# Where the top-k searches of a sparse-attention layer run, and which engine splits the weights beside them

## The chip, the cores and the metric

The kernel runs as one program on one core of a Trainium2 chip. The core has a matrix engine (TensorE, PE in the profile; its weight loads are PEld), a vector engine (VectorE, DVE), an activation engine (ScalarE, ACT), a general engine (GpSimd, POOL) and an engine that issues most transfers (SyncE, SP). Each engine works off its own queue in order, and semaphores hold an instruction back until its inputs and its output's place are free. The metric is the device time of one execution in microseconds (us). Products collect in PSUM, in 128-partition banks; all else lies in SBUF.

## The reference

One step of a two-layer decoder for a prompt of 1024 tokens and eight samples of one token with 1024 past positions each; both share the weights. Layer 0 (state-space and convolution branches) is not touched. Layer 1 is attention over keys that an indexer picks:

```python
def index_scores(qi, wi, ki):
    s = jnp.einsum('bthd,bsd->bths', qi, ki, preferred_element_type=jnp.float32) * IDX_DIM ** -0.5
    return jnp.einsum('bths,bth->bts', jax.nn.relu(s), wi.astype(jnp.float32) * IDX_HEADS ** -0.5)

def dsa_attend(q, qi, wi, q_pos, ki_all, gather_kv, topk):
    scores = index_scores(qi, wi, ki_all)
    ...
    _, idx = lax.top_k(scores, topk)
    ...
    p = jax.nn.softmax(logits, axis=-1)

def odd_out(x, o, z, w_out, ln_g, ln_b):
    out = (o.reshape(b, l, ATTN_WIDTH) * jax.nn.silu(z)) @ w_out
    return layer_norm(ALPHA * x + out, ln_g, ln_b)
```

For each of 1024 prompt queries and 8 sample queries, eight indexer heads score every admissible position, the 256 best are kept, and 16 heads attend to these alone. Queries, keys, values, indexer inputs and a gate z come from one projection of x.

## The kernel before

Nothing is gathered for the prompt. The kernel computes each query's 256th largest score, turns scores into a mask of 0 or a large negative number, and adds it to the logits. So layer 1 has the following stages.

- **Projections.** `mm3` multiplies 128 output columns by a chunk of 344 tokens (there are three, `CH`), in 24 matmuls: for each of eight blocks of the contraction high by high, high by low and low by high, since each fp32 operand is split into a rounded part and the rest. `load_w` fetches a projection's weights in two halves, rounds them on ScalarE (`whi`, L108) and subtracts on VectorE, or on the engine that its argument names (`wlo`, L109). Indexer keys, values and indexer queries (L996 and after, tiles `even` and `odd`) come first, then the attention's queries (`QQ`, eight), keys (`KK`, two) and gates (`ZZ`, eight; called gates below, since a Silu follows).
- **Banks.** The pools `pp`, `pt` and `pm` hold PSUM banks. `QQ` takes `pp`, `KK` and `ZZ` alternate between `pt` and `pp` through `either()`.
- **Scores.** For each block of 128 queries, in the order of `SCORE_ROWS`, and each head and 512 keys, two matmuls (L1033, L1034) fill a `pt` bank, ScalarE takes the Relu into one of two buffers, `eq` and `cum` (L1036), and VectorE multiplies by the head's weight and adds into `S` (L1040).
- **Samples' scores.** `QIP` holds the samples' indexer queries, put in place by 16 small copies (L1058, L1059). Matmuls with past keys collect in three banks `acc` (L1068, L1071), ScalarE takes the Relu (L1074, L1075), and a matmul with `W2` weighs the heads and leaves eight rows in `Ss` (L1086, L1087).
- **Searches.** A search builds the threshold from its top bit down: it counts the scores on one side of a candidate, and keeps or drops the bit. `topk_halves` ("d", query blocks 7, 6, 5) counts on VectorE (L1264) in 16 steps on the upper 16 bits and 16 on the lower. `topk_signs` counts on ScalarE by a sum of signs (L1231) and decides on GpSimd (L1236, L1250 to L1253); it runs as "a" for the blocks 4, 3 and 2, three counts in each of 32 steps, and as "s" for the samples' eight rows of 1025 scores, 32 steps more.
- **Masks.** `masks` (L1299 and after) makes masks on VectorE, for "d", "a" and "s" in this order.
- **Sample logits.** `QS` gathers sample queries by 16 copies (L1151). After each gate projection `sample_keys` fetches past keys and adds 32 matmuls (L1166) to two banks `lg`. `sample_softmax` (from L1558) later adds the mask, which two kinds of matmul (L1565, L1571) spread from 8 rows to 128.
- **Attention** over the blocks 7 down to 0 (logits L1403, maximum L1404, exponential L1408), the gate, and the output projection.

A scheduler fixes each engine's order at build time, from the order of the text and from where tiles come free in their pools. So a bank's pool or an engine's choice moves other instructions too.

Of the kernel before, what the change touches and what calls it, by code (L numbers as in the profile page):

```python
# [880 lines left out]
def layer1(k):  # L881
# [113 lines left out]
    for i in range(4):  # L995
        w = load_w(k, A["W"][QI + i])  # L996
        even, odd = (rq(F32R), rq(F32R)) if i < 3 else (qb(), qb())
        for t0, n in CH:
            p = pp(k)
            mm3(k, p, w, x1, t0, n)  # L1000
            sl = slice(t0, t0 + n)
            nc.scalar.copy(even[0:64, sl], p[0:64])
            nc.vector.tensor_tensor(even[64:128, sl], p[0:64], even[0:64, sl].bitcast(F32), op=ALU.subtract)
            nc.scalar.copy(odd[64:128, sl], p[64:128])
            nc.vector.tensor_tensor(odd[0:64, sl], p[64:128], odd[64:128, sl].bitcast(F32), op=ALU.subtract)
            if t0 + n == T:
# [48 lines left out]
    for h in range(8):  # L1055
        i, j = h // 2, h % 2
        src = qis[64 * j : 64 * j + 64, i, :]
        nc.vector.tensor_copy(QIP[0:64, h : 256 : 80], src[:, 0:8:2])  # L1058
        nc.vector.tensor_copy(QIP[64:128, 8 + h : 256 : 80], src[:, 1:8:2])  # L1059
# [22 lines left out]
    W2 = k.t(tk, [64, 8], F32, "W2")  # L1082
    nc.vector.tensor_tensor(W2, p[:64, :8], c1("bm64")[:64], op=ALU.mult)
    for hf in range(2):
        p = pt(k)
        nc.tensor.matmul(p[:8], W2, rS[:, hf * 512 : hf * 512 + 512], start=True, stop=True)  # L1086
        nc.scalar.copy(Ss[:, hf * 512 : hf * 512 + 512], p[:8])  # L1087
    p = pm(k)
    nc.tensor.matmul(p[:8, 0:8], W2, rS[:, 1024:1032], start=True, stop=True)
    sx = k.t(tk, [8, 8], F32, "sx")  # L1090
    nc.vector.tensor_tensor_reduce(out=sx, in0=p[:8, :8], in1=k.ident[:8, :8], scale=1.0, scalar=0.0,
                                   op0=ALU.mult, op1=ALU.add, accum_out=Ss[:, 1024:1025])

    lg = [pt(k) for _ in range(2)]
# [9 lines left out]
        return pt(k)[:, :344] if turn[0] % 2 else pp(k)  # L1104


    for i in range(8):
        w = load_w(k, A["W"][QQ + i])
        for t0, n in CH:
            p = pp(k)  # L1110
            mm3(k, p, w, x1, t0, n)
            hi, lo = ev(F32R), ev(F32R)
            nc.scalar.copy(hi, p)
            nc.vector.tensor_tensor(lo, p, hi.bitcast(F32), op=ALU.subtract)  # L1114
            for a, x in enumerate((hi, lo)):
                h = 4 * a + 2 * (i % 2)
                nc.sync.dma_start(dq[i // 2, h : h + 2, :, t0 : t0 + n].rearrange("h d t -> (h d) t"), x.bitcast(F32))
            if t0 + n == T:
                nc.scalar.copy(qs[:, i, :], p[:, NP - t0 : n])
    KT = [ra() for _ in range(4)]  # L1120
    for i in range(2):
        w = load_w(k, A["W"][KK + i])
        for t0, n in CH:
            p = either()
            mm3(k, p, w, x1, t0, n)
            sl = slice(t0, t0 + n)
# [21 lines left out]
    for h in range(16):  # L1148
        i, j, g = h // 2, h % 2, h // 4
        r0, o, x = 64 * (g % 2), g // 2 * 256, h % 8  # L1150
        nc.vector.tensor_copy(QS[r0 : r0 + 64, o : o + 256].rearrange("p (f x) -> p f x", f=2)[:, :, x : x + 121 : 40],  # L1151
                              qs[64 * j : 64 * j + 64, i, :].rearrange("p (f c) -> p f c", f=2))
    SL = ra(F32, "ki")[:, :NP]
    ring = [rq() for _ in range(3)]
# [11 lines left out]
                    nc.tensor.matmul(lg[i % 2][r : r + 32, j * 128 : j * 128 + 128], QS[:, o : o + 32],  # L1166
                                     kp[n][:, j, gp * 128 : gp * 128 + 128], start=False, stop=(i > 5), skip_group_check=True)
# [48 lines left out]
    def topk_signs(name, R_, bl):  # L1216
# [10 lines left out]
        for bit in range(31, -1, -1):  # L1227
            cnt = small("cnt", F32)
            for j, (s, rows, w, _) in enumerate(bl):
                jk = k.t(sc_pool, [128, 1032], BF16, "jk" + name, 1)[:rows, :w]  # L1230
                nc.scalar.activation(jk, s, AF.Sign, bias=cand.bitcast(F32)[:, j : j + 1], scale=-1.0, accum_out=cnt[:, j : j + 1])  # L1231

            def fits(out, col, m):

                for j, (_, _, w, _) in enumerate(bl):
                    eng.tensor_scalar(out[:, j : j + 1], cnt[:, j : j + 1], float(w - 2 * TOPK), m(j), op0=ALU.is_le, op1=col)  # L1236

            new = small("cand")
            low, by = small("low"), small("by")
            if bit == 31:  # L1240

                sgn = small("sgn", F32, 1)
                fits(low, ALU.add, lambda j: -1.0)
                fits(sgn, ALU.mult, lambda j: 2.0)
                eng.tensor_scalar(sgn, sgn, -1.0, None, op0=ALU.add)
                eng.tensor_tensor(fstep, fstep, sgn.unsqueeze(1).broadcast_to((R_, 31, n)), op=ALU.mult)
                eng.tensor_copy(by, fstep[:, 30, :])
                eng.tensor_tensor(new, low, by, op=ALU.add)
            else:
# [3 lines left out]
                eng.tensor_tensor(new, low, by, op=ALU.add)  # L1253
# [100 lines left out]
    s8 = [(Ss[:, :1025], 8, 1025, Ss[:, :1025])]  # L1354
# [203 lines left out]
    PT = ra(F32, "ki")[:, :NP].rearrange("p (j r) -> p j r", j=8)  # L1558

    def sample_softmax():  # L1560
        R8 = c1("r128")[:8]
        mx = k.t(right, [128, 1], F32, "mx")
        sm = k.t(right, [128, 1], F32, "sm")
        xm = pop()
        nc.tensor.matmul(xm[:, :1], R8, Ss[:, 1024:1025], start=True, stop=True)  # L1565
        nc.vector.tensor_tensor(nl, nl, xm[:, :1], op=ALU.add)
        m2 = k.t(at, [128, 2], F32, "m2", 1)
        yield
        for hf in range(2):
            lg = pop()  # L1570
            nc.tensor.matmul(lg, R8, Ss[:, hf * 512 : hf * 512 + 512], start=True, stop=True)  # L1571
# [233 lines left out]
```

## Time and profile before

| what | us |
|---|---|
| median of 3 runs | 1693.05 |
| the three runs | 1691.49 to 1696.0 |
| the profiled execution | 1691.48 |
| its span | 1689.3 |
| layer 0 | until about 900 |
| indexer keys, values and indexer queries | 900 to 1006 |
| scores, with a part of `QQ` | 1006 to 1086 |
| rest of `QQ`, `KK` | 1086 to 1190 |
| gates | 1190 to 1292 |
| attention, with output | 1292 to 1660 |
| last transfers | to 1689 |

A busy engine is one with an instruction running; its waits count as idle time and are put down to the instruction that released it. Matmuls overlap in the pipeline, so the distance between two starts is what one costs, not its duration. PEclk is the granted clock, 1.00 being full speed. A row of grouped instructions reads: line, engine, operation, output and inputs with shapes, count, then total and mean duration, then idle time in front and its releasers. A row of waits reads: who waited for whom, total us, times, the longest. A row of busy time by stage gives start and end, length, then each engine's busy time with its count.

### The profile page before, as it was taken

Reading aid. Unit: us, or ns where it says so; the run is one execution under the profiler, and the core shown is the slowest. Engines: PE = TensorE matmul, PEld = TensorE weight load, DVE = VectorE, ACT = ScalarE, POOL = GpSimd, SP = SyncE. Lnnn points to the kernel's source line nnn. Section 1 sums busy time; section 2 is a strip of 40 time slices with the busy share of each in tenths; the row PEclk is TensorE's granted clock in tenths of the full one; section 3 lists DMA queues with packets and bytes.
Section 4 is the critical chain, followed back from the end, with each engine's and each line's share of the span. In section 5 each row is a group of like instructions: output and inputs, shape, how many; then the busy total and the mean of one; then the engine's idle time right before and its main releaser. Section 6 shows DMA issues by size and latency. Waiting matters only on the chain. (4 is left out here: it accounts for less than half of the span.)

```text
span 1689.3 us, 28852 instructions
## 1 busy us (share of the span) xinstructions
PE 1592.6 (94%) x10334; PEld 1433.3 (85%) x10334; DVE 1170.9 (69%) x2484; ACT 871.2 (52%) x1960; POOL 335.7 (20%) x676
## 2 busy tenths in 40 slices
PE   8999989989999998998899999888898899999996
PEld 7999989989999997998889999878887577676674
DVE  4788987460557777766575558999966966565673
ACT  5245523552445565444534546577765755545663
POOL 4000000001222234123422200144361510112120
PEclk9999999999999998999999999999999999999998
DMA  7332243354111155433431214422345424443450
GB/s 235 110 118 62 68 113 101 129 192 140 46 34 63 65 158 184 131 113 103 151 115 53 92 46 132 126 94 95 120 147 183 129 52 117 124 110 89 99 136 37
DMA packets 167090, 186.26 MB, mean 110 GB/s; under 512 B 20484, under 2 KB 131420, under 8 KB 166692
## 3 DMA queue, kind: packets, MB, share of 16 engines
q1 hardware_dynamic: 164436, 178.68, 35.6%
q0 software_dynamic: 1216, 4.37, 0.8%
q8 instruction: 81, 1.33, 0.4%
q10 hardware_dynamic: 1296, 1.38, 0.3%
q14 instruction: 61, 0.50, 0.1%
HBM read 132.43 MB, written 54.05 MB: 110 GB/s over the span
## 5 line engine op out<-in xcount | busy, mean ns | idle before, releaser
L132 PE MATMUL pp<-act,whi 128*128 128x344 f32 x1016 | 329.8, 326 | 12.5 <-ACT act L233 8.1
L134 PE MATMUL pp<-act,wlo 128*128 128x344 f32 x1016 | 331.0, 328 | 10.9 <-DVE wlo L109 10.9
L133 PE MATMUL pp<-act,whi 128*128 128x344 f32 x1016 | 330.1, 325 | 0.9 <-POOL act L726 0.8
L132 PEld LDWEIGHTS pp<-act,whi 128*128 128x128 f32 x1016 | 193.9, 191 | 15.8 <-ACT act L233 8.1
L134 PEld LDWEIGHTS pp<-act,wlo 128*128 128x128 f32 x1016 | 194.1, 191 | 13.5 <-DVE wlo L109 11.8
L133 PEld LDWEIGHTS pp<-act,whi 128*128 128x128 f32 x1016 | 193.9, 191 | 3.2 <-POOL act L726 1.1
L108 ACT CAST whi<-wst 128x512 fp32r<-128x512 f32 x150 | 92.2, 617 | 150.5 <-PE pp L133 68.6
L334 DVE SCALAR_TENSOR_TENSOR uv<-uv,cst,uv 128x1024 f32<-128x1024 f32 x120 | 158.1, 1318 | 2.6
L109 DVE TENSOR_TENSOR wlo<-wst,whi 128x512 fp32r<-128x512 f32 x104 | 71.4, 692 | 100.9 <-ACT whi L108 100.8
L132 PE MATMUL pp<-yh,whi 128*128 128x344 f32 x412 | 135.7, 329 | 5.3 <-DVE ev L1114 3.7
L134 PE MATMUL pp<-yh,wlo 128*128 128x344 f32 x412 | 135.0, 328 | 4.1 <-DVE wlo L109 3.9
L1403 PE MATMUL lg<-w,Q 128*128 128x512 f32 (+3 forms) x384 | 104.5, 378 | 8.7 <-DVE nmx L1404 8.7
L1404 DVE CUSTOM_DVE_ANT_0 P<-lg,w 128x512 f32<-128x512 f32 (+3 forms) x144 | 82.7, 597 | 42.6 <-PE lg L1403 39.0
L109 POOL TENSOR_TENSOR wlo<-wst,whi 128x512 fp32r<-128x512 f32 x46 | 61.0, 1327 | 157.5 <-ACT whi L108 138.2
L1408 ACT ACTIVATE P<-P,mx 128x1024 f32<-128x1024 f32 (+3 forms) x64 | 63.4, 990 | 47.1 <-DVE mx L1407 43.8
L132 PEld LDWEIGHTS pp<-yh,whi 128*128 128x128 f32 x412 | 79.5, 193 | 9.2 <-DVE ev L1114 4.5
L1430 PE MATMUL tr<-cst,P 128*128 128x128 f32 x576 | 85.3, 279 | 1.8 <-DVE yo L1460 1.8
L1430 PEld LDWEIGHTS tr<-cst,P 128*128 128x128 f32 x576 | 64.9, 141 | 25.8 <-issue 18.5
L1403 PEld LDWEIGHTS lg<-w,Q 128*128 128x128 f32 x384 | 64.1, 195 | 26.6 <-DVE nmx L1404 14.5
L134 PEld LDWEIGHTS pp<-yh,wlo 128*128 128x128 f32 x412 | 79.7, 193 | 6.1 <-DVE wlo L109 5.2
L1439 PE MATMUL pv<-ph,V 128*64 128x256 f32 (+1 forms) x640 | 82.3, 372 | 2.0 <-ACT ph L1435 1.6
L1231 ACT ACTIVATE jka<-S,canda 128x640 bf16<-128x640 f32 (+2 forms) x96 | 68.7, 716 | 20.6 <-POOL canda L1253 16.0
(579 smaller groups left out, 3996.9 us busy)
## 6 DMA issues: line engine op xcount, KB each, us to landing
wst<-in_W SPq DMA_DIRECT2D x166, 256.0 KB, 3.0
Q<-dq SPq DMA_DIRECT2D x64, 256.0 KB, 4.1
dq<-ev SPq DMA_DIRECT2D x48, 172.0 KB, 1.8
q<-in_ck SPq DMA_DIRECT2D x64, 128.0 KB, 2.3
vp<-in_cv SPq DMA_DIRECT2D x64, 128.0 KB, 2.2
xst<-in_xT SPq DMA_DIRECT2D x8, 516.0 KB, 10.1
dzb<-ob SPq DMA_DIRECT2D x24, 172.0 KB, 1.8
uv<-dzb SPq DMA_DIRECT2D x8, 516.0 KB, 4.3
```

The costliest lines, as they stand in the source:

```text
L108: nc.scalar.copy(hi, st)
L109: (eng or nc.vector).tensor_tensor(lo, st, hi.bitcast(F32), op=ALU.subtract)
L132: nc.tensor.matmul(out, wh, ah, start=(start and kt == kts[0]), stop=False)
L133: nc.tensor.matmul(out, wh, al, start=False, stop=False)
L134: last = nc.tensor.matmul(out, wl, ah, start=False, stop=(stop and kt == kts[-1]))
L334: nc.vector.scalar_tensor_tensor(out, x, w[:, j : j + 1], y, op0=ALU.mult, op1=ALU.add)
L1231: nc.scalar.activation(jk, s, AF.Sign, bias=cand.bitcast(F32)[:, j : j + 1], scale=-1.0, accum_out=cnt[:, j : j + 1])
L1403: mm = nc.tensor.matmul(lg, Q[:, 4 * a + r, :], KT[g][:, s0 : s0 + m], start=(a == 0), stop=(a == 1))
L1404: nc.vector.tensor_tensor_reduce(out=P[:, s0 : s0 + m], in0=lg, in1=M[tb][:, s0 : s0 + m], scale=-0.125, scalar=BIG, op0=ALU.add, op1=ALU. ...
L1408: nc.scalar.activation(P, P, AF.Exp, bias=mx[:, r : r + 1], scale=-1.0, accum_out=rsum[:, r : r + 1])
L1430: nc.tensor.transpose(p[:, a, r * 128 : r * 128 + 128], Ps[r][:, (sb + a) * 128 : (sb + a) * 128 + 128], k.ident)
L1439: nc.tensor.matmul(pv[64 * u : 64 * u + 64, 256 * pr + c0 : 256 * pr + c1], V[:, sb + a, g * 64 : g * 64 + 64], ph[:, a, c0:c1], start=(sb ...
```

## The change

- The samples' search takes four bits at a time. The score rows are written 16 times over (128 rows: eight samples by 16 candidates, through a `W2` of 128 columns), one count tries 16 candidates, and a matmul with `same`, a 128 x 128 matrix, adds the answers of one sample. That makes 8 steps instead of 32; step n stands behind the n-th query projection. The set-up of its constants is new and stands at the start of layer 1.
- Block 4 becomes a search of its own, "a"; blocks 3 and 2 are "b". They take turns, step by step. GpSimd keeps bit values as integers (`istep`), so the copy in each step goes.
- Where both engines read a bank, ScalarE's reads come first, and VectorE's differences behind them.
- The splits of the weights (`wlo`) of `QQ` and `KK`, and the copies into `QIP` and `QS`, go to GpSimd.
- `QQ` takes its banks from `either()`.
- The mask of the samples has 128 rows, so the softmax's matmuls that spread it go. The block around `xn` moves behind the searches in the text.

The diff, cut to its core:

```diff
@@ set-up at the start of layer 1 @@
+    cix, t8, first, weight, cands = small8("cix"), small8("t8"), small8("first", I32), small8("weight"), small8("cands")
...
+    nc.gpsimd.tensor_tensor(t8, t8, c1("bm128"), op=ALU.mult)
+    nc.vector.tensor_reduce(cix, t8, axis=AX.X, op=ALU.add)
...
+    p = pm(k)[:, :128]
+    nc.tensor.matmul(p, c1("r128")[:8], c1("r128")[:8], start=True, stop=True)
+    nc.scalar.activation(same, p, AF.Copy, scale=t8[:, 3:4])
@@ samples' scores @@
-        nc.vector.tensor_copy(QIP[0:64, h : 256 : 80], src[:, 0:8:2])
+        nc.gpsimd.tensor_copy(QIP[0:64, h : 256 : 80], src[:, 0:8:2])
...
+    W2 = ev()[:64, :128]
...
-        nc.scalar.copy(Ss[:, hf * 512 : hf * 512 + 512], p[:8])
+        nc.scalar.copy(Ss[:, hf * 512 : hf * 512 + 512], p)
@@ search of the samples @@
+    def topk_samples():
...
+        for n in range(8):
+            cnt, fit, d = one("cnt"), one("fit"), one("dig")
+            nc.scalar.activation(jk[:, :1025], Ss[:, :1025], AF.Sign, bias=cand.bitcast(F32), scale=-1.0, accum_out=cnt)
+            eng.tensor_scalar(fit, cnt, float(1025 - 2 * TOPK), None, op0=ALU.is_le)
+            p = pm(k)[:, :1]
+            nc.tensor.matmul(p, same, fit, start=True, stop=True)
+            nc.scalar.copy(d, p)
...
+            yield base
@@ projections @@
     for i in range(8):
-        w = load_w(k, A["W"][QQ + i])
+        w = load_w(k, A["W"][QQ + i], eng=nc.gpsimd)
         for t0, n in CH:
-            p = pp(k)
+            p = either()
             mm3(k, p, w, x1, t0, n)
             hi, lo = ev(F32R), ev(F32R)
             nc.scalar.copy(hi, p)
+            if t0 + n == T:
+                nc.scalar.copy(qs[:, i, :], p[:, NP - t0 : n])
             nc.vector.tensor_tensor(lo, p, hi.bitcast(F32), op=ALU.subtract)
...
-            if t0 + n == T:
-                nc.scalar.copy(qs[:, i, :], p[:, NP - t0 : n])
+        ts = next(ss)
     KT = [ra() for _ in range(4)]
     for i in range(2):
-        w = load_w(k, A["W"][KK + i])
+        w = load_w(k, A["W"][KK + i], eng=nc.gpsimd)
@@ the other searches and the masks @@
-                eng.tensor_copy(low, fstep[:, max(bit - 1, 0), :])
-                eng.tensor_tensor(low, cand, low, op=ALU.subtract)
+                eng.tensor_tensor(low, cand, istep[:, max(bit - 1, 0), :], op=ALU.subtract)
...
-    a, d = blocks(ACT_ROWS), blocks(DVE_ROWS)
-    ta = topk_signs("a", 128, a)
+    a, b, d = blocks(ACT_ROWS[:1]), blocks(ACT_ROWS[1:]), blocks(DVE_ROWS)
+    sa, sb = topk_signs("a", 128, a), topk_signs("b", 128, b)
+    for n in range(32):
+        ta, tb = next(sa), next(sb)
...
-    ts = topk_signs("s", 8, s8)
     masks("d", 128, d, td)
     masks("a", 128, a, ta)
-    masks("s", 8, s8, ts)
+    masks("b", 128, b, tb)
+    masks("s", 128, [(Ss[:, :1025], 128, 1025, Ss[:, :1025])], ts)
@@ sample_softmax @@
-            nc.tensor.matmul(lg, R8, Ss[:, hf * 512 : hf * 512 + 512], start=True, stop=True)
...
-            nc.vector.tensor_tensor(x, x, lg, op=ALU.add)
+            nc.vector.tensor_tensor(x, x, Ss[:, hf * 512 : hf * 512 + 512], op=ALU.add)
```

How the scheduler puts it. On TensorE, in the last part of the scores, before (L1033 and L1034 are the scores, `pp` is a query projection):

```order
L1033 MATMUL pt_10417<-ki_9191,q_9757 128x384
L1034 MATMUL pt_10417<-ki_9192,q_9757 128x384
L132 MATMUL pp_10930<-yh_8243,whi_10858 128x344
L133 MATMUL pp_10930<-yb_8244,whi_10858 128x344
L134 MATMUL pp_10930<-yh_8243,wlo_10859 128x344
L132 MATMUL pp_10930<-yh_8221,whi_10864 128x344
L133 MATMUL pp_10930<-yl_8222,whi_10864 128x344
L134 MATMUL pp_10930<-yh_8221,wlo_10865 128x344
L1033 MATMUL pt_10423<-ki_9191,q_9758 128x384
L1034 MATMUL pt_10423<-ki_9192,q_9758 128x384
L132 MATMUL pp_10930<-yh_8225,whi_10864 128x344
```

After, from the last pair of scores on (now L1073 and L1074) through the samples' sums to the first matmul of the next projection:

```order
L1073 MATMUL pt_10478<-ki_9234,Q_9903 128x384
L1074 MATMUL pt_10478<-ki_9235,Q_9903 128x384
L1130 MATMUL pm_10571<-q_10553,ev_10563 128x8
L1108 MATMUL pt_10502<-w_10505,q_10484 64x128 x8
L1108 MATMUL pt_10502<-w_10506,q_10484 64x128 x8
L1108 MATMUL pt_10503<-w_10527,q_10484 64x128 x8
L1108 MATMUL pt_10503<-w_10528,q_10484 64x128 x8
L1127 MATMUL pt_10565<-q_10553,ev_10563 128x512
L1127 MATMUL pt_10568<-q_10553,ev_10563 128x512
L1139 MATMUL pt_10575<-ev_10577 128x512
L1139 MATMUL pt_10576<-ev_10577 128x512
L132 MATMUL pt_10593<-yh_8237,whi_10583 128x344
```

Before, the projections' matmuls stand between the score pairs to the end; now pairs follow each other, and the projections stand behind the sums.

On ScalarE at the same place, before, from one of the last Relus (L1036) to the samples' Relus (L1074) and the search "a":

```order
L1036 ACTIVATE eq_10432<-pt_10429 128x384
L1119 COPY qs_9165<-pp_10930 128x8
L1036 ACTIVATE cum_10438<-pt_10435 128x384
L1074 ACTIVATE q_10510<-pt_10459 64x512
L1231 ACTIVATE jka_12796,cnta_12791<-S_9951,canda_12789 128x384
L1231 ACTIVATE jka_12813,cnta_12812<-S_9951,canda_12798 128x640
L1074 ACTIVATE q_10510<-pt_10460 64x512
L1231 ACTIVATE jka_12815,cnta_12812<-S_9951,canda_12798 128x512
L1231 ACTIVATE jka_12817,cnta_12812<-S_9951,canda_12798 128x384
L1113 CAST ev_10999<-pp_10974 128x344
```

After, from the last Relu of the scores (now L1076) past the samples' Relus (L1114), the copies to `Ss` (L1128), and steps of both searches:

```order
L1076 ACTIVATE cum_10481<-pt_10478 128x384
L1297 ACTIVATE jka_13164,cnta_13163<-S_9994,canda_13145 128x640
L1297 ACTIVATE jkb_13001,cntb_12998<-S_9994,candb_12996 128x384
L1297 ACTIVATE jka_13185,cnta_13184<-S_9994,canda_13166 128x640
L1114 ACTIVATE q_10553<-pt_10502 64x512
L1297 ACTIVATE jka_13206,cnta_13205<-S_9994,canda_13187 128x640
L1297 ACTIVATE jkb_13026,cntb_13025<-S_9994,candb_13003 128x512
L1297 ACTIVATE jka_13227,cnta_13226<-S_9994,canda_13208 128x640
L1297 ACTIVATE jkb_13028,cntb_13025<-S_9994,candb_13003 128x384
L1114 ACTIVATE q_10553<-pt_10503 64x512
L1128 COPY Ss_9995<-pt_10565 128x512
L1297 ACTIVATE jka_13248,cnta_13247<-S_9994,canda_13229 128x640
```

Search steps have moved ahead of the samples' Relus, and there are two candidates, `canda` and `candb`, in turn.

On GpSimd during the query projections, before, only decisions of the searches "s" and "a":

```order
L1253 TENSOR_TENSOR cands_13788<-lows_13789,bys_13790 8x1
L1236 TENSOR_SCALAR bya_12869<-cnta_12860,fstepa_12757 128x1
L1251 TENSOR_TENSOR lows_13799<-cands_13788,lows_13799 8x1
L1250 CAST lows_13809<-fsteps_13738 8x1
L1253 TENSOR_TENSOR canda_12867<-lowa_12868,bya_12869 128x3
L1251 TENSOR_TENSOR lowa_12884<-canda_12867,lowa_12884 128x3
L1250 CAST lowa_12900<-fstepa_12757 128x3
L1236 TENSOR_SCALAR bys_13800<-cnts_13795,fsteps_13738 8x1
```

After, at a like place:

```order
L1317 TENSOR_TENSOR lowa_13335<-canda_13313,istepa_12915 128x1
L1319 TENSOR_TENSOR candb_13072<-lowb_13073,byb_13074 128x2
L109 TENSOR_TENSOR wlo_10723<-wst_10720,whi_10722 128x512
L1317 TENSOR_TENSOR lowb_13094<-candb_13072,istepb_12964 128x2
L1302 TENSOR_SCALAR bya_13336<-cnta_13331,fstepa_12914 128x1
L109 TENSOR_TENSOR wlo_10837<-wst_10834,whi_10836 128x512
L1319 TENSOR_TENSOR canda_13334<-lowa_13335,bya_13336 128x1
L955 TENSOR_SCALAR poss_10700<-digs_10693 128x1
L1302 TENSOR_SCALAR byb_13095<-cntb_13088,fstepb_12963 128x1
L1227 COPY q_11780<-qs_9165 64x2x4 x2
L1317 TENSOR_TENSOR lowa_13356<-canda_13334,istepa_12915 128x1
L956 TENSOR_SCALAR sgns_10687<-poss_10700 128x1
```

The splits of the weights (L109) now stand between the decisions.

More of the change, by code (lines that the diff above doesn't have):

```diff
@@ L932, in fetch, with signed @@
         nc.sync.dma_start(dst, src[bass.ds(v * rows, rows), :])
+    LEVELS = range(28, -1, -4)
+    small8 = lambda tag, dt=F32: k.t(right, [128, 8], dt, tag)
+    cix, t8, first, weight, cands = small8("cix"), small8("t8"), small8("first", I32), small8("weight"), small8("cands")
+    cix = cix[:, 0:1]
+    for b in range(NS):
+        nc.gpsimd.memset(t8[:, b : b + 1], 8.0 * b)
+    nc.gpsimd.tensor_tensor(t8, t8, c1("bm128"), op=ALU.mult)
+    nc.vector.tensor_reduce(cix, t8, axis=AX.X, op=ALU.add)
+    for col, f in ((0, 0.125), (1, 0.875)):
+        nc.gpsimd.tensor_scalar(t8[:, col : col + 1], c1("rows")[:, col : col + 1], f, None, op0=ALU.mult)
+    nc.gpsimd.tensor_tensor(t8[:, 0:1], t8[:, 0:1], t8[:, 1:2], op=ALU.add)
+    nc.gpsimd.tensor_tensor(cix, t8[:, 0:1], cix, op=ALU.subtract)
+    for n, e in enumerate(LEVELS):
+        nc.gpsimd.memset(weight[:, n : n + 1], float(1 << e))
+    nc.gpsimd.tensor_scalar(cands, weight, cix, None, op0=ALU.mult)
+    def signed(out, d, room, sgn):
+        pos, x, y = room
+        nc.gpsimd.tensor_scalar(pos, d, 8.0, None, op0=ALU.is_ge)
+        nc.gpsimd.tensor_scalar(sgn, pos, 2.0, -1.0, op0=ALU.mult, op1=ALU.add)
+        nc.gpsimd.tensor_scalar(x, pos, -8.0, None, op0=ALU.mult)
+        nc.gpsimd.tensor_tensor(x, x, d, op=ALU.add)
+        nc.gpsimd.tensor_scalar(out, x, sgn, float(1 << 28), op0=ALU.mult, op1=ALU.mult)
+        nc.gpsimd.tensor_scalar(y, pos, -1.0, None, op0=ALU.add)
+        nc.gpsimd.tensor_tensor(out, out, y, op=ALU.add)
+    yi = k.t(right, [128, 1], I32, "yi")
+    signed(first[:, 0:1], cix, (t8[:, 0:1], t8[:, 1:2], yi), t8[:, 2:3])
+    nc.gpsimd.tensor_scalar(yi, cix, 1.0, -float(1 << 23), op0=ALU.is_lt, op1=ALU.mult)
+    nc.gpsimd.tensor_tensor(first[:, 0:1], first[:, 0:1], yi, op=ALU.add)
+    same = k.t(right, [128, 128], F32, "same")
+    nc.gpsimd.tensor_scalar(t8[:, 3:4], cix, 1.0, None, op0=ALU.is_ge)
+    p = pm(k)[:, :128]
+    nc.tensor.matmul(p, c1("r128")[:8], c1("r128")[:8], start=True, stop=True)
+    nc.scalar.activation(same, p, AF.Copy, scale=t8[:, 3:4])
     KIH, KIL = ra(tag="ki"), ra(tag="ki")
@@ L1104, in either @@
         return pt(k)[:, :344] if turn[0] % 2 else pp(k)
+    def topk_samples():
+        eng = nc.gpsimd
+        one = lambda tag, dt=F32: k.t(tk, [128, 1], dt, tag + "s", 2)
+        sgn = k.t(tk, [128, 1], F32, "sgns", 1)
+        step, ups = k.t(tk, [128, 8], F32, "steps", 1), k.t(tk, [128, 8], I32, "upss", 1)
+        cand, base = first[:, 0:1], None
+        jk = ra(BF16, "ki")
+        for n in range(8):
[5 more added lines that the diff above has]
+            nc.scalar.copy(d, p)
+            new = one("base", I32)
+            if n == 0:
+                signed(new, d, (one("pos"), one("room"), one("minus", I32)), sgn)
+                eng.tensor_scalar(step, weight, sgn, None, op0=ALU.mult)
+                eng.tensor_scalar(ups, cands, sgn, None, op0=ALU.mult)
+            else:
+                by = one("by", I32)
+                eng.tensor_scalar(by, d, step[:, n : n + 1], None, op0=ALU.mult)
+                eng.tensor_tensor(new, base, by, op=ALU.add)
+            base = new
+            if n < 7:
+                cand = one("cand", I32)
+                eng.tensor_tensor(cand, base, ups[:, n + 1 : n + 2], op=ALU.add)
+            yield base
+    ss = topk_samples()
     for i in range(8):
-        w = load_w(k, A["W"][QQ + i])
+        w = load_w(k, A["W"][QQ + i], eng=nc.gpsimd)
         for t0, n in CH:
-            p = pp(k)
+            p = either()
             mm3(k, p, w, x1, t0, n)
@@ L1221, in topk_signs @@
         fstep = k.t(tk, [R_, 31, n], F32, "fstep" + name)
+        istep = k.t(tk, [R_, 31, n], I32, "istep" + name)
         for bit in range(31):
@@ L1349, in blocks @@
         return [(S[:, OFF[tb] : OFF[tb] + 128 * (tb + 1)], 128, 128 * (tb + 1), M[tb]) for tb in rows]
-    a, d = blocks(ACT_ROWS), blocks(DVE_ROWS)
-    ta = topk_signs("a", 128, a)
+    a, b, d = blocks(ACT_ROWS[:1]), blocks(ACT_ROWS[1:]), blocks(DVE_ROWS)
+    sa, sb = topk_signs("a", 128, a), topk_signs("b", 128, b)
+    for n in range(32):
+        ta, tb = next(sa), next(sb)
+    xn = pm(k)
+    QX = ev()[:, :128]
+    for gp in range(2):
+        o = gp * 256
+        nc.vector.tensor_reduce(QX[:, gp * 64 : gp * 64 + 64].rearrange("p (f r) -> p f r", f=2),
+                                QS[:, o : o + 256].rearrange("p (f c r) -> p f r c", f=2, c=4), axis=AX.X, op=ALU.add)
+        nc.tensor.matmul(xn[64 * gp : 64 * gp + 64, 0:8], QX[:, gp * 64 : gp * 64 + 64], ks[:, gp, :], start=True, stop=True)
+    xs = k.t(right, [128, 8], F32, "xs")
+    nl = k.t(right, [128, 1], F32, "nl")
+    nc.vector.tensor_tensor_reduce(out=xs, in0=xn[:, 0:8], in1=c1("bm128"), scale=1.0, scalar=0.0,
+                                   op0=ALU.mult, op1=ALU.add, accum_out=nl)
     td = topk_halves("d", d)
-    s8 = [(Ss[:, :1025], 8, 1025, Ss[:, :1025])]
-    ts = topk_signs("s", 8, s8)
     masks("d", 128, d, td)
     masks("a", 128, a, ta)
-    masks("s", 8, s8, ts)
+    masks("b", 128, b, tb)
+    masks("s", 128, [(Ss[:, :1025], 128, 1025, Ss[:, :1025])], ts)
     sc_es.close()
```

51 lines of the change are left out of this document (19 added, 32 removed).

## The prediction

> **What bounds the kernel now.** I read the page's first part, then busy time by stage, the waits of TensorE (PE), and single rows.
>
> ```profile
> PE 1592.6 (94%) x10334; PEld 1433.3 (85%) x10334; DVE 1170.9 (69%) x2484; ACT 871.2 (52%) x1960; POOL 335.7 (20%) x676
> ```
>
> PE has work for 94% of the span, so a change pays where PE stands still or runs slowed. All edited work lies between 900 and about 1320 us; the part that matters is cut here by stage.
>
> ```profile
> core 0: us, PE busy (x) PEld busy (x) DVE busy (x) ACT busy (x) POOL busy (x), PEclk, DMA share, GB/s
> 1006.00:1066.00 60.00, 60.00 (x356) 56.83 (x355) 54.09 (x109) 35.46 (x77) 0.82 (x2) 1.00 0.38 115
> 1066.00:1175.00 109.00, 94.20 (x558) 88.01 (x558) 105.67 (x257) 75.57 (x172) 39.87 (x168) 0.93 0.36 110
> 1175.00:1207.00 32.00, 29.95 (x189) 27.99 (x188) 30.63 (x71) 24.57 (x56) 11.37 (x53) 0.96 0.32 93
> 1207.00:1230.00 23.00, 18.50 (x154) 17.23 (x153) 22.05 (x53) 16.49 (x42) 8.47 (x32) 0.93 0.43 138
> 1230.00:1292.00 62.00, 60.57 (x504) 57.73 (x502) 34.26 (x53) 37.81 (x96) 30.38 (x73) 1.00 0.44 134
> 1292.00:1350.00 58.00, 48.42 (x295) 31.22 (x284) 52.65 (x125) 39.97 (x62) 19.64 (x12) 0.94 0.61 179
> ```
>
> To 1066 PE is full while the index scores run. From 1066 to 1230 it lacks 14.8 + 2.0 + 4.5 = 21.3 us, with a granted clock of 0.93 to 0.96, and there VectorE (DVE) is full: 158 of 164 us. From 1230 to 1292 PE is full again; at the attention's start it lacks 9.6 us, with DVE at 52.7 of 58. The waits from 1086 to 1292 name DVE too:
>
> ```profile
> PE pt L134 <- DVE wlo L109: 5.9, 3, 3.8
> PE pp L134 <- DVE wlo L109: 3.9, 3, 2.5
> PE pp L132 <- DVE ev L1114: 3.4, 2, 2.1
> ```
>
> So taking weight splits, copies and masks off DVE strikes the right engine. The question is what PE then has to do, and when.
>
> **The change, part by part.**
>
> (1) *PE beside the scores.* The prompt's query projections took their banks from pp; now they alternate, and the first wants a pt bank, which the scores and the samples' sums use. In the order, 482 projection matmuls stand between the first and the last score matmul before, and 228 now; the missing 254 come after. Among the scores' instructions, what filled PE is gone. How much that was, shows the row of tile pp alone:
>
> ```profile
> 1006.00:1066.00 60.00, 45.36 (x236) 38.56 (x234) 4.59 (x9) 4.97 (x13) 1.00 0.38 115
> ```
>
> 236 matmuls of 60 us' work were projections. Now PE has 36 of them left there (one and a half chunks of 24) and otherwise waits for the scores' consumers. The 254 cost this pitch:
>
> ```profile
> 1215.47 0.66 PE L134 MATMUL pt<-yh,wlo 128*128 128x344 f32 x1 [3.81 <-DVE wlo L109]
> ...
> 1218.77 0.32 PE L134 MATMUL pp<-yh,wlo 128*128 128x344 f32 x1
> ...
> 1221.77 0.32 PE L132 MATMUL pt<-yh,whi 128*128 128x344 f32 x1
> ```
>
> The last two rows are 19 matmuls apart: 3.00 / 19 = 0.158 us each, so 254 × 0.158 = **40.1 us of cover lost**.
>
> (2) *The scores' end.* The scores run at DVE's pace (54.1 of 60 us). Their last step in before is
>
> ```profile
> 1085.97 0.62 DVE L1040 SCALAR_TENSOR_TENSOR S<-cum,wi,S 128x384 f32<-128x384 f32 x1
> ```
>
> From 1006.5 to there DVE also does these, which the new order puts elsewhere (the splits and copies on GpSimd, POOL; the projections' differences after the scores):
>
> ```profile
> L1114 DVE TENSOR_TENSOR ev<-pp,ev 128x344 fp32r<-128x344 f32 x12 | 6.1, 510 | 1.5 <-ACT ev L1113 1.5
> L109 DVE TENSOR_TENSOR wlo<-wst,whi 128x512 fp32r<-128x512 f32 x8 | 5.5, 686 | 0.0
> L1059 DVE COPY q<-qis 64x4 f32<-64x4 f32 x8 | 1.3, 167 | 0.1
> ```
>
> With as many copies of L1058 as of L1059, 6.1 + 5.5 + 2 × 1.3 = 14.2 us, with 1.5 of waiting. The six halving steps that DVE interleaves stay. Giving back some 3 us to waits on ScalarE (ACT), whose queue now holds search steps between the scores' Relus, the scores end at 1086.5 − 15.7 + 3 = 1074 (1071 to 1081).
>
> (3) *From the scores to the projections.* The first remaining projection now stands on PE behind the samples' score sums, which wait for two ACT Relus (L1114 of the new text), the second behind four steps of the 640 block, one of 512 and two of 384. ACT and POOL rows between 1066 and 1230:
>
> ```profile
> L1231 ACT ACTIVATE jks<-Ss,cands 8x1025 bf16<-8x1025 f32 x32 | 36.8, 1148 | 2.3 <-DVE Ss L1091 1.2 <-POOL cands L1253 0.9
> L1231 ACT ACTIVATE jka<-S,canda 128x640 bf16<-128x640 f32 x19 | 15.6, 821 | 5.1 <-POOL canda L1253 3.3 <-POOL canda L1248 1.8
> L1231 ACT ACTIVATE jka<-S,canda 128x512 bf16<-128x512 f32 x20 | 14.3, 714 | 0.1
> L1231 ACT ACTIVATE jka<-S,canda 128x384 bf16<-128x384 f32 x20 | 12.1, 606 | 2.2 <-DVE S L1040 2.0
> L108 ACT CAST whi<-wst 128x512 fp32r<-128x512 f32 x20 | 12.1, 605 | 0.5 <-PE pp L133 0.5
> L1113 ACT CAST ev<-pp 128x344 fp32r<-128x344 f32 x14 | 6.1, 434 | 5.9 <-PE pp L134 3.3 <-DMA dq<-ev 2.6
> L1074 ACT ACTIVATE q<-pt 64x512 f32<-64x512 f32 x2 | 1.2, 576 | 0.0
> ...
> L1236 POOL TENSOR_SCALAR bya<-cnta,fstepa 128x1 int32<-128x1 f32 x56 | 19.0, 341 | 25.8 <-ACT jka L1231 25.1
> L1253 POOL TENSOR_TENSOR canda<-lowa,bya 128x3 int32<-128x3 int32 x18 | 3.8, 213 | 0.7
> ```
>
> 4 × 0.82 + 0.71 + 2 × 0.61 + 2 × 0.58 = 6.4 us, and about 1.5 for POOL's answers between steps (0.34 + 0.21 each, mostly behind the other search) and PE's own two matmuls. The projections start at 1074 + 8 = **1082** (1077 to 1090).
>
> (4) *From there to the gates' end.* 1260 projection matmuls follow (1006 stood behind the last score before): 199.1 us. The samples' keys come after each gate projection; from one such group to the next:
>
> ```profile
> 1238.64 1.08 PE L1166 MATMUL pt<-q,q 128*32 128x128 f32 x32
> ...
> 1251.22 0.43 PE L1166 MATMUL pt<-q,q 128*32 128x128 f32 x8
> ```
>
> 12.58 − 72 × 0.158 = 1.2 us, eight times 9.6. So PE could be done at 1082 + 199.1 + 9.6 = 1290.7, against 1292.2 now: what DVE's stalls cost before (21.3 us and the clock) and the cover lost nearly cancel. What decides are the new stalls, L.
>
> (5) *L.* Two engines now carry what paces PE. ACT has, up to the first gate chunk, by the rows above 19 × 0.82 + 29 × 0.71 + 30 × 0.61 + 8 × 1.15 + 17 × 0.61 + 42 × 0.43 + some 3 = 95 us beside 684 × 0.158 = 108 us of PE: dense, in a fixed order in which each evacuation of a PE bank stands behind search steps that wait for POOL. The sample steps shrink from 32 to 8, and reading a bank first on ACT takes away stalls behind DVE; both help. POOL gets the 17 splits still to come:
>
> ```profile
> L109 POOL TENSOR_TENSOR wlo<-wst,whi 128x512 fp32r<-128x512 f32 x46 | 61.0, 1327 | 157.5 <-ACT whi L108 138.2
> ```
>
> 17 × 1.33 = 22.6 us, each ahead of search steps in POOL's queue, for which ACT and then PE's banks wait. The eight new sample matmuls (L1161) also make PE wait for POOL, with the next projection queued behind. No row shows this chain: between 0 and all 22.6 us exposed I take half, 11.3, since two searches take turns and two kinds of bank (pp, pt) lie between ACT and PE. To it comes the restart after the sparse stage. In the fence of part 1, after 3.81 us of standing, eleven matmuls take 1218.77 − 1215.47 = 3.30 us instead of 1.74: 1.6 lost. L = **13** (3 to 26); the gates end at 1303.7, 11.5 later than now.
>
> The Trainium skill, "TensorE: Matmul & The Clock Gate", Part 1, says that the array falls to half clock after an idle window of about 3.4 us and needs as long of steady work to come back. By it one cold start costs 1.7 us, as the row says; it would also make the sparse score stage a slow one, which is a rival below.
>
> (6) *The attention's start.* Masks of ACT's rows and of the samples, such as the scan below, still stand on DVE there. They can now run beside the gates, where DVE has 28 of 62 us free, since their searches end before the gates.
>
> ```profile
> PE lg L1403 <- DVE nmx L1404: 6.8, 3, 4.7
> ...
> L1331 DVE TENSOR_TENSOR_SCAN cum<-eq 8x1025 f32<-8x1025 f32 x1 | 2.3, 2276 | 0.0
> ...
> L1571 PE MATMUL po<-Ss,cst 8*128 8x512 f32 x4 | 2.2, 640 | 0.0
> ```
>
> PE lacks 9.6 us there, 3.5 more by its clock (58 × 0.06), and does 2.2 us of sample matmuls that go: at most 15. ACT's table load and the first logits still come in their turn, and DVE stays near full, so I take half: **−7.5** (−4 to −11).
>
> (7) *Small edits.* The new set-up on POOL, DVE, PE and ACT near 915 stands ahead of work on PE's path: 0 to 2, I take 1. The wider sample rows (128 partitions instead of 8) have the duration of their 1025 columns. The moved xn block lies under the gates.
>
> **Sum.** 1082 + 199.1 + 9.6 + 13 = 1303.7, less 1292.2 = +11.5; −7.5; +1: +5.0 on the profiled execution's 1691.5, so 1696.5. The shown runs have a median of 1693.05, 1.6 above that execution; I go between: **1697**.
>
> **Rivals.**
> - *ACT and POOL become the bound* (slower). If all 22.6 us of splits are exposed, the searches run into the gates, where their evacuations stand behind the last step. L = 26: +24.5 − 7.5 + 1 = +18: about 1710. It decides from L = 13 upward. For it: ACT at 95 of 108 us in series with POOL. Against: POOL is busy for only 40 of 109 us in 1066 to 1175.
> - *The freed DVE pays in full* (faster). Scores end at 1072, PE starts at 1080, L = 3: gates end at 1291.7; with −10 at the attention: −10.5, about 1682. For it: nearly all of PE's waits named DVE. Against: the cover of part 1.
> - *PE runs the score stage slowed.* Of the 60 us before, 60 − 236 × 0.158 = 22.7 were no projections. At half speed that is 45 of 60, and with the 36 projections left about 57 of 68: PE close to DVE's pace and late for each Relu. +5: 1702. The trace has no such stage; its lower clocks (0.93, 0.94) stand beside whole waits. The same section of the Trainium skill's clock-gate page would have it so, if gaps between score pairs count as idle.
>
> **How the numbers follow.** Forecast 0.39, ACT and POOL 0.24, the freed DVE 0.28, the slowed scores 0.09. The range 1682 to 1711 runs from one rival to the other. 0.3% of 1693, about what can be told from no change here, is 5.1 us: below 1688 is faster, above 1698 slower. The forecast splits into 0.03 faster, 0.22 same, 0.14 slower, lying close to the edge; the first rival is slower; the second 0.24 faster, 0.04 same; the third 0.03 same, 0.06 slower. Faster 0.27, same 0.29, slower 0.44.
>
> **What would show it.** In the new profile PE should be about half busy from 1006 to 1074 and its first chunk after the scores should start near 1082. The waits from there to 1200 should name ACT's casts and POOL's splits, no longer DVE; the last search step should come before the first gate's Silu, the masks before the gates' end, and the first exponential some 4 us after it. If PE is dense in the score stage, or starts its projections before 1077, part 1 or 3 is wrong; if PE has no stalls after 1082, L is.

## The result, and the profile after

| | before | after |
|---|---|---|
| median, us | 1692.27 (4 runs, 1690.64 to 1696.0) | 1713.01 (4 runs, 1709.14 to 1718.63) |
| ratio | | 1.0123, 95% interval 1.0096 to 1.015 |
| profiled execution | 1691.48 | 1716.39 |

The change is slower by about 21 us; the forecast was 1697, the upper end of its range 1711. First busy time by stage of the changed kernel, with the columns of the table before:

```profile
1006.00:1066.00 60.00, 45.75 (x167) 30.60 (x165) 54.62 (x110) 34.92 (x74) 9.08 (x34) 0.82 0.15 45
1066.00:1175.00 109.00, 95.71 (x550) 90.14 (x549) 105.26 (x244) 76.60 (x200) 66.04 (x223) 0.90 0.37 111
1175.00:1207.00 32.00, 28.08 (x178) 27.52 (x177) 30.83 (x71) 19.79 (x55) 15.27 (x45) 1.00 0.34 106
1207.00:1230.00 23.00, 18.73 (x107) 17.95 (x106) 22.51 (x31) 15.30 (x39) 14.40 (x23) 0.93 0.26 85
1230.00:1292.00 62.00, 62.00 (x517) 59.95 (x517) 33.96 (x61) 12.13 (x25) 0.00 (x0) 1.00 0.57 168
1292.00:1350.00 58.00, 53.35 (x405) 43.64 (x404) 23.28 (x69) 28.41 (x45) 7.62 (x4) 1.00 0.63 183
```

In the score stage (first row) PE now issues 167 matmuls instead of 356. From 1066 to 1230 PE lacks 21.5 us, as before (21.3), and DVE, which the change was to relieve, is as full as before: 158.6 of 164 us. From 1230 PE is full, at a time when before 62 us of gates were left; now there are 92. The waits of PE from 1085 to 1322:

```profile
PE pp L132 <- DVE ev L1190: 10.4, 5, 3.1
PE pt L134 <- DVE wlo L109: 2.4, 1, 2.4
PE pp L132 <- ACT whi L108: 2.0, 1, 2.0
PE pp L132 <- DVE w L1211: 1.7, 1, 1.7
PE pm L1161 <- POOL fits L1159: 0.7, 1, 0.7
```

14.5 of these 17.2 us name DVE: the query differences (L1190), the key differences (L1211), a split of the gates' weights. (A difference is what is left of a product after its rounded part; DVE takes it from the PSUM bank, and only after that is the bank free for another projection.) Single rows of PE, the first projection after the scores, a later one, and the last keys of the gates:

```profile
1084.98 0.66 PE L132 MATMUL pt<-yh,whi 128*128 128x344 f32 x1
...
1088.50 0.32 PE L132 MATMUL pt<-yh,whi 128*128 128x344 f32 x1
...
1320.96 1.08 PE L1242 MATMUL pt<-q,q 128*32 128x128 f32 x32
```

The gates end at 1322.0. One line's instructions on DVE: the scores' additions and the key differences, after and (third row) before, each with count, durations, and first and last start:

```profile
L1080 DVE SCALAR_TENSOR_TENSOR S<-cum,wi,S x40: 343/746/784, 975.0 to 1074.3; 128x512 f32<-128x512 f32 x24, 128x384 f32<-128x384 f32 x8, 128x256 f32<-128x256 f32 x4, 128x128 f32<-128x128 f32 x4
L1211 DVE TENSOR_TENSOR w<-pp,w x6: 509/515/520, 1207.9 to 1226.5; 64x344 fp32r<-64x344 f32 x6
L1133 DVE TENSOR_TENSOR w<-pp,w x6: 508/515/520, 1168.9 to 1192.4; 64x344 fp32r<-64x344 f32 x6
```

The scores end 12 us earlier, the key differences 34 us later. As the waits show, PE gets a bank for its next projection by these differences.

### The profile page after: what moved, and what is told of

Read it like the earlier page. It is cut to its first block, busy times and chain, and to the rows that moved or that the text cites. A ratio compares the mean times of both kernels' runs of the same rounds, so it can differ in the third digit from the quotient of the medians.

```text
span 1714.6 us, 28851 instructions
## 1 busy us (share of the span) xinstructions
PE 1608.4 (94%) x10346; PEld 1439.7 (84%) x10346; DVE 1160.8 (68%) x2439; ACT 845.2 (49%) x1921; POOL 356.8 (21%) x705
## 4 chain that ended last, share of the span: by engine, by line
PE 73%; DVE 14%; ACT 3%; issue 3%; DMA 3%; POOL 2%; SPq 1%; DVEq 0%; ACTq 0%; POOLq 0%
PE pp L134 11%; PE pp L132 11%; PE pp L133 11%; PE po L1569 5%; DVE jkd L1330 5%; PE pv L1517 4%; PE lg L1481 3%; PE tr L1508 3%; PE pt L132 3%; PE pt L134 3%; PE pt L133 3%; PE pt L625 2%; PE pt L353 2%; DVE S L1080 2%; ACT cft L351 1%
## 5 line engine op out<-in xcount | busy, mean ns | idle before, releaser
L109 DVE TENSOR_TENSOR wlo<-wst,whi 128x512 fp32r<-128x512 f32 x84 | 57.7, 693 | 123.6 <-ACT whi L108 123.1
L109 POOL TENSOR_TENSOR wlo<-wst,whi 128x512 fp32r<-128x512 f32 x66 | 86.5, 1312 | 213.2 <-ACT whi L108 202.0
L132 PE MATMUL pp<-yh,whi 128*128 128x344 f32 x316 | 104.1, 330 | 14.0 <-DVE ev L1190 10.4
L134 PE MATMUL pp<-yh,wlo 128*128 128x344 f32 x316 | 102.5, 324 | 0.0
L351 ACT ACTIVATE cft<-cw,own 128x80 f32<-128x80 f32 x256 | 66.2, 348 | 20.9 <-PE pt L353 12.2
L132 PEld LDWEIGHTS pp<-yh,whi 128*128 128x128 f32 x316 | 60.9, 193 | 17.2 <-DVE ev L1190 11.8
L134 PE MATMUL pt<-yh,wlo 128*128 128x344 f32 x220 | 71.9, 327 | 2.4 <-DVE wlo L109 2.4
```

The costliest lines, as they stand in the source:

```text
L109: (eng or nc.vector).tensor_tensor(lo, st, hi.bitcast(F32), op=ALU.subtract)
L132: nc.tensor.matmul(out, wh, ah, start=(start and kt == kts[0]), stop=False)
L134: last = nc.tensor.matmul(out, wl, ah, start=False, stop=(stop and kt == kts[-1]))
L351: nc.scalar.activation(wv[:, :, :, ch, :], taps2, AF.Copy, scale=own[:, ch : ch + 1])
```

## The experiments

**Which engine holds PE after the scores?** Theory D: DVE. Theory A, the prediction's: ACT and POOL. Half of search b left out:

```diff
-        ta, tb = next(sa), next(sb)
+        ta = next(sa)
+        if n % 2 == 0:
+            tb = next(sb)
```

> The changed kernel, with every second step of search b left out (16 of 32, so the masks of blocks 3 and 2 are wrong). Theory D: VectorE's queue is the same, so within 4 us of the change, 1709 to 1717. Theory A: ScalarE loses 16 x (0.72 + 0.61) = 21 us and GpSimd about 18 us of a chain that sets the pace, so 15 to 25 us faster, about 1693.

Measured 1715.82, ratio 1.0125 (1.0094 to 1.0155): 32 counts less in ACT's and POOL's chain bought nothing, as theory D expected. The splits back on DVE:

```diff
-        w = load_w(k, A["W"][QQ + i], eng=nc.gpsimd)
+        w = load_w(k, A["W"][QQ + i])
```

(the same for `KK`)

> The changed kernel, with the weight splits of the query and key projections back on VectorE. Theory D: 17 splits x 0.61 us more stand in VectorE's full queue, so about 10 us slower, about 1723. Theory A: GpSimd is rid of 17 x 1.29 = 22 us that stood among its search decisions, so about 10 us faster, about 1703.

Measured 1715.01, 1.0137 (1.0115 to 1.0158): neither theory's time. This speaks against theory A, since the kernel is no faster with POOL rid of the splits. D's 10 us more did not come either; a likely reason is that the scheduler then put part of the masks behind the last key difference (one scan ahead of it instead of two), which takes work out of DVE's queue there. Half of DVE's lower steps left out:

```diff
-        for bit in range(15, -1, -1):
+        for bit in range(15, 7, -1):
```

> The changed kernel, with 8 of the 16 lower steps of VectorE's search left out (so the masks of the query blocks 7, 6 and 5 are cut off coarser). Theory D (VectorE's queue, which runs without a gap from the last score to the last key difference, holds the banks that TensorE needs): VectorE has 24 counts and their small steps less, about 33 us, so TensorE's stalls mostly go and the gates end about 20 to 28 us earlier: about 1690, against 1713 for the change. Theory A (ScalarE and GpSimd in series pace TensorE, as the prediction had it): no work of theirs goes, so 1710 to 1716.

Measured 1706.19, 1.0077 (1.0055 to 1.0098): 7 us, a third of what D expected. Busy time by stage shows why:

```profile
1086.00:1130.00 44.00, 39.97 (x245) 39.40 (x244) 42.73 (x91) 28.24 (x75) 28.77 (x87) 0.96 0.40 121
1130.00:1175.00 45.00, 38.78 (x227) 38.21 (x226) 42.98 (x96) 28.57 (x78) 26.34 (x80) 0.92 0.41 126
1175.00:1230.00 55.00, 52.44 (x355) 51.15 (x354) 29.04 (x48) 37.30 (x97) 26.79 (x69) 1.00 0.34 110
```

The counts left out stood late in the queue. Up to 1175 DVE is as full as in the change and PE stalls as there; only behind that is PE dense. So the same search was held back as a whole, with nothing left out:

```diff
+            if bit == 25:
+                nc.vector.tensor_scalar(zero, ks[:, 1, 0:n], 1e30, None, op0=ALU.is_equal)
+                nc.vector.tensor_tensor(held, cand, zero.bitcast(U32), op=ALU.bitwise_or)
+                cand = held
```

> The changed kernel, with VectorE's search held back after its sixth upper step until the last key projection (an operation reads ks); no work is left out. In the order no count stands between the last score and the last key difference (81 in the change). Theory D (VectorE's turn is what TensorE waits for): from the first projection after the scores to the first Silu of the gates 141 us become 112 to 118, close to TensorE's own 108. Theory B (the three ev buffers and their stores, or ScalarE with GpSimd, hold TensorE): 130 to 141 us. The whole time says little, since the search then comes beside the gates and in the attention: 1700 to 1730 by both.

```profile
1086.00:1130.00 44.00, 44.00 (x281) 44.00 (x281) 6.21 (x12) 35.12 (x96) 31.39 (x110) 0.99 0.50 151
1130.00:1175.00 45.00, 45.00 (x289) 45.00 (x289) 6.51 (x14) 37.10 (x102) 29.39 (x98) 1.00 0.49 150
...
L1251 ACT ACTIVATE ev<-pt x12: 452/458/462, 1199.8 to 1312.2; 128x344 f32<-128x344 f32 x12
```

The same row of the change:

```profile
L1251 ACT ACTIVATE ev<-pt x12: 449/458/458, 1226.2 to 1317.3; 128x344 f32<-128x344 f32 x12
```

PE has no gap from 1086 to 1175, with ACT and POOL doing the changed kernel's searches beside it. From its first projection (1084.1) to the first Silu (1199.8) are 115.7 us, against 1226.2 − 1085.0 = 141.2 in the change. This settles it for D: neither ACT and POOL nor the `ev` buffers (theory B) hold PE once DVE's counts are out of the way. The whole is 1744.26, 1.0283 of before (1.0263 to 1.0304), and slower than the 1730 expected: the search comes beside the gates and the attention's start, where, from 1292 to 1350, DVE is busy for 56.0 of 58 us and PE for 37.1.

**Why is DVE as full as before?** It kept its search, and got what stood among the scores before. Between the last score and the last key difference the order has 81 counts and 24 query differences in the change, 58 and 12 before. The projections had left the scores; two edits could be the reason, and both were undone, W2 (128 columns) going beside QIP:

```diff
-    QIP = rq()[:, :256]
+    QW = rq()
+    QIP, W2 = QW[:, :256], QW[:64, 256:384]
...
-    W2 = ev()[:64, :128]
...
-            p = either()
+            p = pp(k)
```

> The changed kernel with the query projections' banks from pp again, and with W2 in free columns beside QIP, so that it no longer takes one of the three ev buffers; in the order 480 projection matmuls stand among the scores again (228 in the change) and 12 of VectorE's query differences before the last score (none). All else of the change stays. Theory D with the cover of the scores restored: TensorE comes out of the scores with 1008 instead of 1260 matmuls to do, about 40 us less, minus some 10 us that VectorE needs longer in the scores; gates end about 25 to 40 us earlier, so 1675 to 1688, faster than before the change too. Theory A: ScalarE and GpSimd have the same work in about the same order, so at most 10 us faster than the change, 1703 to 1713.

Measured 1685.35, ratio to before 0.9954 (0.9931 to 0.9977): 28 us below the change and 7 below the kernel before.

```profile
1006.00:1066.00 60.00, 59.74 (x351) 55.74 (x349) 54.48 (x106) 34.32 (x77) 11.64 (x14) 1.00 0.38 114
...
L1211 DVE TENSOR_TENSOR w<-pp,w x6: 508/515/520, 1171.0 to 1189.8; 64x344 fp32r<-64x344 f32 x6
```

PE is full in the score stage again and the last key difference starts at 1189.8 instead of 1226.5. Next, each edit by itself. The bank alone undone in the change:

> The changed kernel with the query projections' banks from pp again, W2 still in an ev buffer. In the order the interleaving does not come back: 240 projection matmuls among the scores, no query difference before the last score. Theory I (two locks, the bank from pt and W2 in one of three ev buffers, each of which alone keeps the projections behind the samples' sums): as slow as the change, 1709 to 1717. Rival (the bank alone is the cause): about 1685, as with both undone.

Measured 1711.65, 1.0127 (1.0095 to 1.016): as slow as the change. The bank alone changed in the kernel before (`p = pp(k)` to `p = either()`):

> The kernel before, with only the query projections' banks changed to either(). In the order 228 projection matmuls are left among the scores, and between the last score and the last key difference VectorE has 83 counts, 24 query differences and 20 splits (58, 12 and 12 before). Theory I: VectorE's full queue reaches the last key difference 25 to 30 us later, so 1715 to 1725, as slow as the whole change or slower. Rival (the loss is from other edits): 1690 to 1696.

Measured 1720.17, 1.0171 (1.0143 to 1.02). And W2 alone, still of 8 columns, `W2 = ev()[:64, :8]` in the kernel before:

> The kernel before, with only W2 (still 64 x 8) taken from the three ev buffers instead of a place of its own. In the order 240 projection matmuls are left among the scores. Theory I: as with either(), 1712 to 1725. Rival: a small buffer in another place costs nothing, 1690 to 1696.

Measured 1722.87, 1.0174 (1.0141 to 1.0206). Either edit costs some 28 to 30 us by itself, both together no more. The `ev` ring has three buffers; `zero` holds one and W2 the second until the samples' sums, so a projection, which takes two (`hi` and `lo`), can't be read out of its bank before. The traces agree: with W2 there, the first query difference starts at 1075.3, behind the last of the sums (from 1071.6); in the kernel before at 1006.9.

**Can the rest be improved?** All of these have both edits undone. Block 5 moved from DVE's search to ACT's:

```diff
-ACT_ROWS = (4, 3, 2)
+ACT_ROWS = (5, 4, 3, 2)
-DVE_ROWS = (7, 6, 5)
+DVE_ROWS = (7, 6)
```

> The kernel with both locks undone, and query block 5 moved from VectorE's search to ScalarE's: a has the blocks 5 and 4, b the blocks 3 and 2 (one buffer for both searches' unused output, for room). VectorE has 44 counts instead of 61 between the last score and the last key difference, but two scans of masks more; ScalarE has 32 counts of 768 more, about 30 us. Theory D (VectorE's full queue is what is left to bound this stretch): 8 to 12 us faster than with both locks undone, about 1675. Rival (ScalarE with GpSimd becomes the bound): 1685 to 1700.

Measured 1690.75, 0.9993 (0.9977 to 1.0009): not theory D's time but the rival's. The gates end 12 us earlier (1278.5), but ACT's search then ends at 1252 and its masks at 1292. From the gates' end to the end of the span are 405 us instead of 392, and at the attention's start PE has 47.9 of 58 us instead of 51.4:

```profile
1292.00:1350.00 58.00, 47.92 (x291) 32.52 (x289) 42.78 (x101) 36.45 (x59) 24.15 (x14) 0.90 0.48 122
```

The splits of queries and keys back on DVE:

> Both locks undone (the query projections' banks from pp, W2 beside QIP), and the weight splits of the query and key projections back on VectorE. In the order VectorE has 55 counts and 12 splits between the last score and the last key difference, 61 and 3 with the splits on GpSimd; 55 x 1.2 + 12 x 0.61 = 73 us against 75. Theory D: the same within 4 us, 1681 to 1689. Theory A: GpSimd's queue loses 22 us of splits, so 5 to 10 us faster, 1675 to 1680.

Measured 1681.42, 0.994 (0.9922 to 0.9958): no dearer there than on POOL. DVE's lower steps held back until the keys are done, all 16, or from the fourth on (with `bit == 12` in place of 15):

```diff
+            if bit == 15:
+                nc.vector.scalar_tensor_tensor(held, ks[:, 1, 0:n], 0.0, kept, op0=ALU.mult, op1=ALU.add)
+                kept = held
```

> Both locks undone, and all 16 lower steps of VectorE's search made to start after the last key projection (a small operation reads ks, times 0). VectorE has 30 counts instead of 61 between the last score and the last key difference, 37 us less, and TensorE is no longer held by it there; but the counts come beside the gates, where VectorE has about 42 of 62 us of work, so the masks end about 15 to 25 us later than 1269. Theory D: gates end 12 to 20 us earlier (1271 to 1279), part of it given back at the attention's start: 1670 to 1680. Theory A: ScalarE and GpSimd keep their pace, 1682 to 1690.

> As h2_late15, but only from the fourth lower step on: 39 counts between the last score and the last key difference, 26 us less than with both locks undone. Theory D: gates end 10 to 15 us earlier (1276 to 1281), the masks by about the end of the gates, little given back: 1670 to 1677. Theory A: 1682 to 1690.

Measured 1700.9 (1.005, 1.0033 to 1.0067) and 1682.95 (0.9952, 0.9936 to 0.9968), neither within what theory D expected. PE is dense from 1130 to 1175 as expected, but now waits beside the gates for splits of their weights (`wlo`) that stand behind counts, and at the attention's start for `nmx`; the waits for query differences (`ev`) lie before 1130. With all 16 held back:

```profile
PE pp L132 <- DVE ev L1190: 7.1, 2, 5.1
PE lg L1485 <- DVE nmx L1486: 6.6, 4, 4.0
PE pp L134 <- DVE wlo L109: 6.5, 3, 3.6
...
PE pt L134 <- DVE wlo L109: 3.3, 2, 2.4
```

So the gates' splits went to POOL, which is idle there, the others to DVE, and the steps were held back from the fourth on:

> Both locks undone; the splits of the query and key projections on VectorE, those of the gates on GpSimd, which has little left to do there; VectorE's lower steps from the fourth on start after the last key projection. VectorE has 40 counts and 9 splits between the last score and the last key difference (61 and 3 with both locks undone only), and no split stands behind a count beside the gates. Theory D: gates end 10 to 14 us earlier than with both locks undone (1277 to 1281), and the masks are done by the gates' end: 1670 to 1677, below every kernel so far. Rival (what VectorE no longer holds up is held by ScalarE and GpSimd, or given back at the attention's start): 1680 to 1686.

Measured 1678.09, ratio 0.9919 (0.9901 to 0.9937), 1 us above what was expected. Of all the kernels here only the next has a lower median, by 0.9 us, less than the spread of either. The longest wait of this one is new, at the gates' end:

```profile
PE pm L1431 <- DVE ev L1429: 13.2, 1, 13.2
```

That is the block around `xn`, behind DVE's masks. Put back ahead of the gates:

> The best kernel so far (k3_best, 1678), with the block around xn back ahead of the gates, as in the kernel before. Theory: its two reductions no longer stand behind VectorE's masks at the end of the gates, so the wait of 13.2 us goes; what the masks delay at the attention's start stays in part, so 6 to 12 us faster: 1666 to 1672. Rival (TensorE then waits as long for the same masks at the first logits): 1676 to 1680.

```profile
PE lg L1485 <- DVE nmx L1486: 15.2, 7, 11.9
```

Measured 1677.18, 0.9886 (0.9867 to 0.9905): the rival. The wait moves to the first logits, which stand behind the same masks. From 1006 to 1292 DVE is busy for 258 of 286 us; of the rest, some 15 are waits between 1086 and 1180, mostly for ACT's copies of the keys. Whether counts put into those waits would bring the masks forward, or only less work on DVE would, was not tried.

## Why the prediction was wrong

The forecast gave slower the largest chance (0.44), and slower it is; the time, 1713, lies above the whole range (1682 to 1711). Its steps, against the profile:

- *Cover lost* (part 1), 40 us: right, and it is the cause of the slowdown. Undoing it alone in the change gives 28 us back; the last step of the scores then starts at 1085.7 instead of 1074.3, which takes 11 of the 40. That W2's place is a second lock was not seen; the prediction put all of it on the bank. PE was not about half busy there, as forecast, but for 45.8 of 60 us, with 167 matmuls at a granted clock of 0.82.
- *Scores' end* 1074: 1074.9 (the last step starts at 1074.3). *First projection* 1082: 1085.0, with 3.6 us of waiting for the samples' second Relu behind ACT's searches, as part 3 had it.
- ***L*** (part 5), 13 us: this step failed. 1322.0 − 1085.0 − 199.1 − 9.6 = 28.3. The prediction let the stalls behind DVE (21.3 us before) go, made ACT and POOL the engines that pace PE and priced POOL's splits. But the waits after 1085 still name DVE. Half of search b left out, and the splits moved back, gained nothing; and with DVE's search held back, PE runs without a gap beside ACT and POOL. DVE paces it. Its load after the scores was never added up, though the order of the change and the rows of before allow it: 23 counts more ahead of the last key difference at about 1.2 us from start to start, 12 differences more at 0.4, two blocks' masks, against 9 splits and the copies less. From the last score to the last key difference DVE takes 152 us (1074.9 to 1227.0) without waiting for any other engine, and 106 before, also without a wait. The 12 query differences that left the scores came back behind them, and, the keys now being later in the order, counts and masks that stood behind the last key difference stand ahead of it.
- *The attention's start*, −7.5: from the gates' end to the span's end 1714.6 − 1322.0 = 392.6, 397.1 before: −4.5, within the bounds of part 6. The masks end before it (1262) and the first exponential starts 4 us after it (1326.1), as forecast.
- *Sum*: +3.0 for the first projection, +15.3 for L, +3.0 for the attention, on 1696.5, make 1717.8; the profiled execution has 1716.4. One us of the difference is the forecast's own term for the set-up (part 7), which the times read from the profile already hold.
- *Rivals*: ACT and POOL as the bound gave a time, 1710, near the one measured, by the wrong engine: that is luck. The slowed score stage did happen (granted clock 0.82) and cost nothing there: the scores ended when forecast. Of the freed DVE nothing came, since it was not freed up to the last key difference; with the projections back among the scores the rest of the change is worth −7 us.

## What to carry to other kernels

When work moves off a full engine, add up what that engine has left in each stage between the points where others wait for it: here DVE left the scores 12 us earlier and then had 46 us more to do before the last key difference. A buffer taken from a short ring, or a bank from another pool, can hold back everything that shares it, whatever its size: compare the orders for what left a stage, and look for every lock before undoing one. Work that fills an engine's gaps has a price in that engine's order: here a search between the reads of PSUM banks set when the banks came free.

## What the runs showed of the hardware that was not expected

PE's clock fell without a long wait. In the changed kernel's score stage, in stretches of 10 us, with the waits for the Relus from 1006 to 1066:

```profile
1016.00:1026.00 10.00, 8.30 (x28) 4.17 (x28) 9.37 (x17) 7.57 (x15) 0.00 (x0) 1.00 0.01 2
1026.00:1036.00 10.00, 7.77 (x26) 5.14 (x26) 9.07 (x16) 6.50 (x14) 0.00 (x0) 0.83 0.00 0
1036.00:1046.00 10.00, 7.18 (x22) 4.59 (x23) 9.88 (x24) 4.55 (x11) 0.00 (x0) 0.73 0.00 1
...
PE pt L1073 <- ACT eq L1076: 6.7, 12, 1.3
PE pt L1073 <- ACT cum L1076: 3.9, 6, 1.3
```

No single wait for the Relus between 1006 and 1066 is longer than 1.3 us, and the one longer wait (3.0 us, for POOL's copies) comes only at 1058.6. The granted clock still drops, to 0.83 and 0.73 in these tens of 26 and 22 matmuls; in the ten before, of 28, it is 1.00. In the kernel before, 57 to 64 matmuls run in each of the tens from 1006 to 1066, at 1.00. The prediction had such a stage as its least likely rival (0.09). The projections then start slowly: twelve matmuls from 1084.98 to 1088.50 take 3.5 us instead of 1.9. That is not shown to come from the scores: in between, from 1069.6 to 1077, sixty matmuls of the samples ran at 0.89, and the wait of 3.6 us ends at 1081.8, only four matmuls ahead of these twelve.
